# Modulation summed over whole rows of 2048 values, loaded two columns ahead, with its small sums once per block of 16

## The chip, the cores and the metric

The kernel runs on one core of one Trainium2 chip. The metric is the device time of one execution in microseconds. Engines are named as the profile names them: PE (TensorE, PEld is its weight load), DVE (VectorE), ACT (ScalarE), POOL (GpSimd) and SP (SyncE, which issues the loads).

## The reference

An encoder of two layers works on x of 256 tokens by 2048 features. Each layer is modulated by a vector c of 2048 values (adaLN):

```python
c_act = jax.nn.silu(c)
for l in range(DEPTH):
    mod = c_act @ ada_w[l] + ada_b[l]                     # 2048 -> 6 * 2048
    sh1, sc1, g1, sh2, sc2, g2 = jnp.split(mod, 6)
    h = rmsnorm(x, norm_mix_g[l]) * (1.0 + sc1) + sh1
    proj = h @ w_in[l] + b_in[l]
    y = concat(rglru(...), attention(...), hyena(...), mlstm(...))   # the mixer, four groups of 512 features
    x = x + g1 * (y @ w_out[l])
    h = rmsnorm(x, norm_ffn_g[l]) * (1.0 + sc2) + sh2
    x = x + g2 * swiglu(h, ffn_w1[l], ffn_w3[l], ffn_w2[l])
return rmsnorm(x, final_g)
```

All arrays are float32. The modulation alone reads 2 x 2048 x 12288 weights, 201 MB; the large products read the rest.

## The kernel before

The stream x lies in SBUF as 16 tiles of 128 features by 256 tokens. All large weights come from HBM in pieces of 128 x 1024 values (512 KB) through SP's queue into three `raw` buffers. Each piece is split exactly into two float32r parts: ACT makes `hi` (L335), DVE makes `lo` = raw - hi (L336), with three buffers of each. PE then runs 24 matmuls of 128 x 256 per piece: `hi` by `hi` of the activation (L372), `hi` by its `lo` (L373), and `lo` by its `hi` (L374). The result is collected in the banks `a`. DVE adds it to the stream, times a column of the modulation (`x`, L1097, two tiles per bank). ACT squares x (`sq`), PE sums the squares (`ss`, L475), and the root comes back spread over the partitions as `rb` (L482). The normed input `h` is made tile by tile: DVE multiplies x, a factor `g` and `rb` (L495), ACT adds the shift and rounds (L497), DVE makes the rest (L498).

The modulation has 192 columns: 2 layers, 6 parts (0 to 5 are sh1, sc1, g1, sh2, sc2, g2), 16 columns of 128 features each. A column is 128 dot products of 2048 values, one to a partition, of a block of `ada` weights with `cb`, which holds silu(c) on every partition. DVE does it with a multiplication that accumulates along the row (L423; the profile shows a `DVE_READ_ACCUMULATOR` behind each). Before, a column is done in two halves of 1024 values, each with a load of 512 KB of its own. A load and its sum stand together in the program:

```python
self.load(t, self.d["ada"][l, b, :, h * 1024:(h + 1) * 1024])
nc.vector.scalar_tensor_tensor(t, t, 1.0, self.cb[:, h * 1024:(h + 1) * 1024], ALU.mult, ALU.mult,
                               accum_out=self.acc[l][:, b, h:h + 1])
```

The halves go into two buffers `ada` of 4 KB a partition, and at the start of the program two of three go into spare tiles of another pool, `ad`. After the second half one small sum per column (L428) adds the halves and the bias; for parts 2 and 5 two small sums per 16 columns do (L432, L433). The norm's factor g = (1 + sc) * norm weight is one more small instruction per tile (L493).

The columns are strewn among the weights: after each piece `ada(rate)` is called, with the rates `RATES` in half columns a piece, for w_in, the first w1 and w3, the rest of the feed-forward part, and w_out. The first 32 columns (layer 0, parts 0 and 1) are needed at the start, where the spectra of the hyena filters are made. A call `modc` asks for a column and makes what is still missing.

A scheduler puts the instructions of each engine into order from a simulated timeline, and each engine then works in that order. `load` holds a load behind the weights that were asked for before it (`issue_after`).

Of the kernel before, what the change touches and what calls it, by code (L numbers as in the profile page):

```python
# [18 lines left out]
P = 128  # L19
DEPTH = 2  # L20
# [24 lines left out]
def _in_columns():  # L45
    """Source column of every column of the 42 plain blocks, in the kernel's order."""
# [22 lines left out]
def _out_rows():  # L69
    """Source row of w_out for every row of the mixed features, in the kernel's order c, d, a, b."""  # L70
    r = [1024 + np.arange(1024), np.arange(512)]
    for i in range(4):
        r += [512 + 64 * i + np.arange(64), 512 + 64 * (i + 4) + np.arange(64)]
    return np.concatenate(r)
# [5 lines left out]
# ---------------------------------------------------------------- constants of the shapes  # L80
def _constants():
# [36 lines left out]
    # behind the permutation of the rotation: rows 2 i and 2 i + 1 spread over the halves of tile i  # L118
# [38 lines left out]
# ---------------------------------------------------------------- layout of the inputs  # L157
# [67 lines left out]
# ---------------------------------------------------------------- the program  # L225
# pairs of column blocks that are worked on together while their input is still being made
IN_LEAD, OUT_LEAD, FFN_LEAD = 4, 5, 3
# half columns of the modulation per piece of weights, by layer: w_in, first w1 and w3, the rest of the FFN, w_out
# [3 lines left out]
class Lazy:  # L232
    """A list of n tiles, each made when it is first asked for, in their order."""
# [13 lines left out]
class Net:  # L247
    NRAW, NHL, NADA = 3, 3, 2
    # 2 KB tiles, by what they hold: a tag's tiles get their places in the order of the program
# [57 lines left out]
    def load(self, dst, src):  # L307
        """A load that does not run ahead of the weights that were asked for before it."""
# [47 lines left out]
    def product(self, banks, acts, m):  # L356
        """bank[:, b*T:(b+1)*T] = W[:, block b].T @ act, for m blocks of 128 columns in each bank.
        acts: per row tile, [hi | lo]. Several banks take turns chunk by chunk."""
# [18 lines left out]
    def products(self, n, lead, acts):  # L377
        """The banks of n pairs of column blocks in turn; the first `lead` of them are worked on together."""
# [8 lines left out]
    def split(self, dst, src):  # L387
        """dst (float32r) = [hi | lo] of src, exactly."""
        self.nc.scalar.activation(dst[:, :T], src, AF.Copy)  # L389
        self.nc.vector.tensor_tensor(dst[:, T:], src, dst[:, :T].bitcast(F32), ALU.subtract)  # L390

# [1 line left out]
    def ada_init(self, order):  # L393
# [11 lines left out]
        self.acc = [self.cp.tile([P, 96, 2], F32, name=f"acc{l}") for l in range(DEPTH)]  # L405
        self.ada_items = [(l, b, h) for l, b in order for h in range(2)]
        self.ada_at = 0
        self.ada_left = 0.0

    def ada(self, n, wide=False):  # L410
        """The next n half columns of the modulation; wide: with more of them under way."""
        nc = self.nc
        self.ada_left += n
        while self.ada_left >= 0.999 and self.ada_at < len(self.ada_items):
            self.ada_left -= 1
            l, b, h = self.ada_items[self.ada_at]
            self.ada_at += 1
            if wide and self.ada_at % 3:
                t = self.pair("ad")
            else:  # L420
                t = self.wp.tile([P, 1024], F32, tag="ada", name=self.nm("ada"), bufs=self.NADA)
            self.load(t, self.d["ada"][l, b, :, h * 1024:(h + 1) * 1024])
            nc.vector.scalar_tensor_tensor(t, t, 1.0, self.cb[:, h * 1024:(h + 1) * 1024], ALU.mult, ALU.mult,  # L423
                                           accum_out=self.acc[l][:, b, h:h + 1])
            if h == 0:
                continue
            if b // 16 not in (2, 5):
                nc.vector.scalar_tensor_tensor(self.mod[l][:, b:b + 1], self.acc[l][:, b, 0:1], self.acc[l][:, b, 1:2],  # L428
                                               self.pc(l, "ada_b", b), ALU.add, ALU.add)
            elif b % 16 == 15:  # L430
                m = self.mod[l][:, b - 15:b + 1]
                nc.vector.tensor_tensor(m, self.acc[l][:, b - 15:b + 1, 0], self.acc[l][:, b - 15:b + 1, 1], ALU.add)  # L432
                nc.vector.tensor_tensor(m, m, self.pc(l, "ada_b", b - 15, 16), ALU.add)  # L433

    def modc(self, l, j, k):
        """Column k of part j; parts 2 and 5 come as a whole."""
        b = j * 16 + k
        while self.ada_at <= self.ada_items.index((l, b | 15 if j in (2, 5) else b, 1)):
            self.ada(1, wide=l == 0 and j < 2)
        return self.mod[l][:, b:b + 1]  # L440

# [1 line left out]
    def rsqrt(self, v, n):  # L443
        """v ** -0.5 of a tiny tile: a start from ScalarE, one Newton step on it."""
# [743 lines left out]
```

## Time and profile before

| | us |
|---|---|
| time, median of 3 runs | 2658.27 |
| lowest and highest run | 2654.43, 2661.93 |
| span of the profiled execution (its own time, from the first to the last instruction) | 2648.9 |
| PE busy in it | 2523.5 |
| DVE busy | 1811.4 |
| ACT busy | 1158.7 |

The span leaves out what lies around the instructions, so the timed runs stand 5.5 to 13.0 us above it. A busy PE counts its matmuls at their own pace, with the granted clock in them; an engine that waits off PE's path costs nothing.

### The profile page before, as it was taken

The numbers are of one execution on the slowest core, as the hardware profiler recorded it, in microseconds if no ns is written. First come the engines' busy times: TensorE is split into PE (matmuls) and PEld (weight loads), VectorE is DVE, ScalarE is ACT, GpSimd is POOL, SyncE is SP. The second block draws the span as 40 slices with busy tenths as digits, with TensorE's granted clock in tenths as the row PEclk, the third lists the DMA queues.
The fourth block names the chain that finished last, engine by engine and source line by source line (L and its number), as shares of the span: only waits on it lengthen the run. The fifth ranks groups of instructions, "written<-read, shape, count | busy, mean of one in ns | idle before, by whom it ended". The sixth has DMA issues, their size and how long they took to land.

```text
span 2648.9 us, 47579 instructions
## 1 busy us (share of the span) xinstructions
PE 2523.5 (95%) x19410; PEld 2404.3 (91%) x19410; DVE 1811.4 (68%) x2778; ACT 1158.7 (44%) x1669; POOL 161.9 (6%) x142
## 2 busy tenths in 40 slices
PE   6889989798999999999998999999899999999998
PEld 3469989598999999999998898989899999999998
DVE  7888788778767666766677767777766454454445
ACT  4444455444443344334434445654444334433443
POOL 2101010021000000000020111002000000000001
PEclk9789999898999999999999999999999999999999
DMA  8787878467887778887776766658688656556654
GB/s 281 267 308 267 263 255 295 173 244 241 278 281 272 263 267 266 271 265 269 254 257 231 254 219 229 212 167 271 223 282 270 192 183 183 180 181 189 183 180 148
DMA packets 180752, 630.19 MB, mean 238 GB/s; under 512 B 20162, under 2 KB 20371, under 8 KB 180531
## 3 DMA queue, kind: packets, MB, share of 16 engines
q1 hardware_dynamic: 177076, 620.84, 70.5%
q10 hardware_dynamic: 3456, 6.29, 0.6%
q8 instruction: 152, 2.49, 0.4%
q14 instruction: 68, 0.56, 0.1%
HBM read 618.67 MB, written 8.39 MB: 237 GB/s over the span
## 4 chain that ended last, share of the span: by engine, by line
PE 58%; DMA 8%; DVE 5%; issue 4%; ACT 1%; SPq 0%; POOL 0%; DVEq 0%; POOLq 0%; ACTq 0%
PE a L374 19%; PE a L373 19%; PE a L372 19%; DMA ada<-in_ada 6%; DVE lo L336 2%; DMA raw<-in_w_in 1%; DMA raw<-in_w 1%; DVE ada L423 1%; ACT hi L335 0%; DMA raw<-in_w_out 0%; DVE x L1097 0%; DVE h L495 0%; DVE h L498 0%; SPq L324 0%; PE m L812 0%
## 5 line engine op out<-in xcount | busy, mean ns | idle before, releaser
L335 ACT ACTIVATE hi<-raw 128x1024 fp32r<-128x1024 f32 (+2 forms) x780 | 810.8, 1041 | 1181.4 <-PE a L373 698.5
L336 DVE TENSOR_TENSOR lo<-raw,hi 128x1024 fp32r<-128x1024 f32 (+2 forms) x780 | 948.1, 1218 | 425.1 <-ACT hi L335 419.9
L374 PE MATMUL a<-h,lo 128*128 128x256 f32 x4192 | 1204.2, 288 | 26.7 <-DVE lo L336 26.6
L372 PE MATMUL a<-h,hi 128*128 128x256 f32 x4192 | 1206.0, 288 | 10.2 <-ACT hi L335 5.5
L373 PE MATMUL a<-h,hi 128*128 128x256 f32 x4192 | 1206.3, 288 | 1.7 <-DVE h L498 1.7
L374 PEld LDWEIGHTS a<-h,lo 128*128 128x128 f32 x4192 | 815.1, 195 | 40.6 <-DVE lo L336 30.2
L372 PEld LDWEIGHTS a<-h,hi 128*128 128x128 f32 x4192 | 815.7, 195 | 28.5 <-ACT hi L335 8.9
L373 PEld LDWEIGHTS a<-h,hi 128*128 128x128 f32 x4192 | 815.5, 195 | 8.1 <-DVE h L498 2.8
L423 DVE SCALAR_TENSOR_TENSOR ada<-ada,cb 128x1024 f32<-128x1024 f32 x341 | 425.1, 1247 | 340.7 <-DMA ada<-in_ada 339.9
L374 PE MATMUL a<-g,lo 128*128 128x256 f32 x1408 | 399.7, 284 | 2.9 <-DVE lo L336 2.8
L373 PE MATMUL a<-g,hi 128*128 128x256 f32 x1408 | 399.2, 283 | 0.0
L372 PE MATMUL a<-g,hi 128*128 128x256 f32 x1408 | 399.1, 283 | 0.0
L374 PEld LDWEIGHTS a<-g,lo 128*128 128x128 f32 x1408 | 271.0, 193 | 4.0 <-DVE lo L336 4.0
L372 PEld LDWEIGHTS a<-g,hi 128*128 128x128 f32 x1408 | 271.1, 193 | 0.0
L373 PEld LDWEIGHTS a<-g,hi 128*128 128x128 f32 x1408 | 271.0, 192 | 0.0
L466 POOL TENSOR_TENSOR sq<-sq,sq 128x256 f32<-128x256 f32 x65 | 81.6, 1255 | 1694.4 <-issue 1399.7
L1097 DVE SCALAR_TENSOR_TENSOR x<-a,mod,x 128x256 f32<-128x256 f32 x128 | 55.8, 477 | 5.5 <-PE a L374 5.4
L423 DVE SCALAR_TENSOR_TENSOR ad<-ad,cb 128x1024 f32<-128x1024 f32 x43 | 54.5, 1274 | 0.1
L389 ACT ACTIVATE g<-s 128x256 fp32r<-128x256 f32 x88 | 35.9, 408 | 35.2 <-DVE s L1109 35.1
L497 ACT ACTIVATE h<-h,mod 128x256 fp32r<-128x256 f32 x64 | 29.4, 501 | 42.0 <-DVE h L495 28.5
L464 ACT ACTIVATE sq<-x 128x256 f32<-128x256 f32 x75 | 29.2, 413 | 24.5 <-DVE x L1097 24.3
L374 PE MATMUL a<-yc,lo 128*128 128x256 f32 x128 | 36.8, 288 | 1.0 <-DVE lo L336 1.0
(247 smaller groups left out, 2017.7 us busy)
## 6 DMA issues: line engine op xcount, KB each, us to landing
raw<-in_w SPq DMA_DIRECT2D x496, 512.0 KB, 4.6
ada<-in_ada SPq DMA_DIRECT2D x341, 512.0 KB, 5.7
raw<-in_w_in SPq DMA_DIRECT2D x168, 512.0 KB, 4.9
raw<-in_w_out SPq DMA_DIRECT2D x64, 512.0 KB, 5.7
ad<-in_ada SPq DMA_DIRECT2D x43, 512.0 KB, 6.3
raw<-in_w SPq DMA_DIRECT2D x32, 384.0 KB, 3.1
spectra<-sl ACTq DMA_DIRECT2D x24, 256.0 KB, 7.0
spec<-spectra SPq DMA_DIRECT2D x24, 256.0 KB, 6.7
```

Of the source, the lines that this page charges most:

```text
L335: self.nc.scalar.activation(hi[:, :n], t[:, :n], AF.Copy)
L336: self.nc.vector.tensor_tensor(lo[:, :n], t[:, :n], hi[:, :n].bitcast(F32), ALU.subtract)
L372: mm(o, hi[:, c], a[:, :T], start=first and b == 0, stop=False, skip_group_check=True)
L373: mm(o, hi[:, c], a[:, T:], start=False, stop=False, skip_group_check=True)
L374: mm(o, lo[:, c], a[:, :T], start=False, stop=last, skip_group_check=True)
L389: self.nc.scalar.activation(dst[:, :T], src, AF.Copy)
L423: nc.vector.scalar_tensor_tensor(t, t, 1.0, self.cb[:, h * 1024:(h + 1) * 1024], ALU.mult, ALU.mult, accum_out=self.acc[l][:, b, h:h + 1])
L464: nc.scalar.activation(t, self.x[k], AF.Square)
L466: nc.gpsimd.tensor_tensor(self.sq, self.sq, t, ALU.add)
L497: nc.scalar.activation(h[:, :T], t, AF.Identity, bias=sh)
L1097: self.nc.vector.scalar_tensor_tensor(self.x[k], ps[:, b * T:(b + 1) * T], g, self.x[k], ALU.mult, ALU.add)
```

## The change

A column is now one load of 1 MB (128 x 2048) and one sum over 2048 values. There are three buffers of 8 KB a partition, and the load of a column is asked for two columns ahead of its sum. The tiles `ad` and the argument `wide` are gone. Only layer 0's parts 0 and 1 keep one small instruction per column: for part 1 it makes the factor (`gain`) at once, for part 0 the shift. Everywhere else the bias is added once per 16 columns, and for the scale parts (1 and 4) a second instruction makes the 16 factors; L493 is gone. The order of the columns is now by whole parts, apart from layer 0's parts 1 and 0. `modc` waits for the whole block of 16 where it is made at once. The scratch size given to the compiler makes room in SBUF.

```diff
-    NRAW, NHL, NADA = 3, 3, 2
+    NRAW, NHL, NADA = 3, 3, 3
...
-        self.acc = [self.cp.tile([P, 96, 2], F32, name=f"acc{l}") for l in range(DEPTH)]
-        self.ada_items = [(l, b, h) for l, b in order for h in range(2)]
-        self.ada_at = 0
+        self.acc = [self.cp.tile([P, 96], F32, name=f"acc{l}") for l in range(DEPTH)]
+
+        self.gain = {(l, j): self.cp.tile([P, 16], F32, name=f"gain{l}{j}") for l in range(DEPTH) for j in (1, 4)}
+        self.bias1 = self.cp.tile([P, 16], F32, name="bias1")
+        nc.vector.tensor_scalar(self.bias1, self.pc(0, "ada_b", 16, 16), 1.0, None, ALU.add)
+        self.ada_items = order
+        self.ada_at = self.ada_got = 0
         self.ada_left = 0.0
-
-    def ada(self, n, wide=False):
-        """The next n half columns of the modulation; wide: with more of them under way."""
+        self.ada_tiles = {}
+
+    def ada(self, n):
+
         nc = self.nc
         self.ada_left += n
-        while self.ada_left >= 0.999 and self.ada_at < len(self.ada_items):
-            self.ada_left -= 1
-            l, b, h = self.ada_items[self.ada_at]
+        while self.ada_left >= 1.999 and self.ada_at < len(self.ada_items):
+            self.ada_left -= 2
+            while self.ada_got < min(len(self.ada_items), self.ada_at + self.NADA):
+                l, b = self.ada_items[self.ada_got]
+                t = self.wp.tile([P, D], F32, tag="ada", name=self.nm("ada"), bufs=self.NADA)
+                self.load(t, self.d["ada"][l, b])
+                self.ada_tiles[self.ada_got] = t
+                self.ada_got += 1
+            l, b = self.ada_items[self.ada_at]
+            t = self.ada_tiles.pop(self.ada_at)
             self.ada_at += 1
...
-            nc.vector.scalar_tensor_tensor(t, t, 1.0, self.cb[:, h * 1024:(h + 1) * 1024], ALU.mult, ALU.mult,
-                                           accum_out=self.acc[l][:, b, h:h + 1])
...
+            acc, mod = self.acc[l], self.mod[l]
+            nc.vector.scalar_tensor_tensor(t, t, 1.0, self.cb, ALU.mult, ALU.mult, accum_out=acc[:, b:b + 1])
+            j, k = b // 16, b % 16
+            if l == 0 and j < 2:
+                if j:
+                    nc.vector.scalar_tensor_tensor(self.gain[l, j][:, k:k + 1], acc[:, b:b + 1], self.bias1[:, k:k + 1],
+                                                   self.pc(l, "nmix", k), ALU.add, ALU.mult)
+                else:
+                    nc.vector.tensor_tensor(mod[:, b:b + 1], acc[:, b:b + 1], self.pc(l, "ada_b", b), ALU.add)
+            elif k == 15:
+                c = slice(j * 16, j * 16 + 16)
+                nc.vector.tensor_tensor(mod[:, c], acc[:, c], self.pc(l, "ada_b", j * 16, 16), ALU.add)
+                if j in (1, 4):
+                    nc.vector.scalar_tensor_tensor(self.gain[l, j], mod[:, c], 1.0, self.pc(l, "nmix" if j == 1 else "nffn", 0, 16),
+                                                   ALU.add, ALU.mult)
...
         b = j * 16 + k
-        while self.ada_at <= self.ada_items.index((l, b | 15 if j in (2, 5) else b, 1)):
-            self.ada(1, wide=l == 0 and j < 2)
-        return self.mod[l][:, b:b + 1]
...
+        while self.ada_at <= self.ada_items.index((l, b if l == 0 and j < 2 else b | 15)):
+            self.ada(2)
+        return self.gain[l, j][:, k:k + 1] if j in (1, 4) else self.mod[l][:, b:b + 1]
...
-                g = self.yp.tile([P, 1], F32, tag="g", name=self.nm("g"))
-                nc.vector.scalar_tensor_tensor(g, sc, 1.0, self.pc(l, gname, k), ALU.add, ALU.mult)
...
-        order = [(l, j * 16 + k) for l in range(DEPTH) for js in ((1, 0), (2,), (4, 3), (5,)) for k in range(16) for j in js]
+        order = [(0, j * 16 + k) for k in range(16) for j in (1, 0)]
+        order += [(l, j * 16 + k) for l in range(DEPTH) for j in ((1, 0) if l else ()) + (2, 4, 3, 5) for k in range(16)]
...
-    nc = bacc.Bacc("TRN2", target_bir_lowering=False, num_devices=1)
+    nc = bacc.Bacc("TRN2", target_bir_lowering=False, num_devices=1, dynamic_dma_scratch_size=1024)
```

The scheduler's order moves with it. On SP, in layer 0's mixer at the rate of one half column a piece, these loads stand in a row before:

```order
L313 DMA ada_1667<-in_ada 128x1024
L324 DMA raw_1670<-in_w_in 128x1024
L313 DMA ada_1700<-in_ada 128x1024
L324 DMA raw_1703<-in_w_in 128x1024
L313 DMA ada_1733<-in_ada 128x1024
L324 DMA raw_1736<-in_w_in 128x1024
```

and these in the changed kernel, at about the same place:

```order
L324 DMA raw_1549<-in_w_in 128x1024
L313 DMA ada_1579<-in_ada 128x2048
L324 DMA raw_1582<-in_w_in 128x1024
L324 DMA raw_1612<-in_w_in 128x1024
L313 DMA ada_1642<-in_ada 128x2048
L324 DMA raw_1648<-in_w_in 128x1024
```

The same bytes go in one load after every second piece. In layer 0's attention DVE makes the rotated `aq` in steps that alternate with PE (L758 and L762 to L767 before, L767 and L771 to L776 after). Before, DVE has there:

```order
L758 SCALAR_TENSOR_TENSOR aq_3998<-p_3710,par,m_4047 128x512
L423 SCALAR_TENSOR_TENSOR ada_5002,acc_151<-ada_5002,cb 128x1024
L428 SCALAR_TENSOR_TENSOR mod_149<-acc_151,par 128x1
L493 SCALAR_TENSOR_TENSOR g_6233<-mod_149,par 128x1
L762 TENSOR_TENSOR aa_4050<-m_4052,rope_3988 128x512
L423 SCALAR_TENSOR_TENSOR ada_5066,acc_151<-ada_5066,cb 128x1024
L767 TENSOR_TENSOR aq_3998<-aq_3998,aa_4050 128x512
L758 SCALAR_TENSOR_TENSOR aq_3999<-p_3710,par,m_4057 128x512
L762 TENSOR_TENSOR aa_4060<-m_4062,rope_3988 128x512
L767 TENSOR_TENSOR aq_3999<-aq_3999,aa_4060 128x512
```

and after, for the same steps:

```order
L767 SCALAR_TENSOR_TENSOR aq_3787<-p_3515,par,m_3836 128x512
L336 TENSOR_TENSOR lo_4664<-raw_4661,hi_4663 128x1024
L771 TENSOR_TENSOR aa_3839<-m_3841,rope_3777 128x512
L336 TENSOR_TENSOR lo_4697<-raw_4694,hi_4696 128x1024
L767 SCALAR_TENSOR_TENSOR aq_3788<-p_3515,par,m_3846 128x512
L431 SCALAR_TENSOR_TENSOR ada_4754,acc_151<-ada_4754,cb 128x2048
L776 TENSOR_TENSOR aq_3787<-aq_3787,aa_3839 128x512
L771 TENSOR_TENSOR aa_3849<-m_3851,rope_3777 128x512
L776 TENSOR_TENSOR aq_3788<-aq_3788,aa_3849 128x512
```

Two half sums stood between the steps, and one whole sum and two `lo` stand there now; on PE 65 weight matmuls stand between the first step of these (L755, now L764) and the scores (L783, now L792), where 18 stood. At the change from layer 0 to layer 1 DVE has before:

```order
L423 SCALAR_TENSOR_TENSOR ada_14885,acc_152<-ada_14885,cb 128x1024
L432 TENSOR_TENSOR mod_150<-acc_152 128x16
L336 TENSOR_TENSOR lo_14870<-raw_14867,hi_14869 128x1024
L433 TENSOR_TENSOR mod_150<-mod_150,par 128x16
L1097 SCALAR_TENSOR_TENSOR x<-a_14773,mod_149,x 128x256 x2
L336 TENSOR_TENSOR lo_14945<-raw_14942,hi_14944 128x1024
L423 SCALAR_TENSOR_TENSOR ada_15002,acc_152<-ada_15002,cb 128x1024
L478 TENSOR_SCALAR v_14903<-ss_14896 128x2
```

and after:

```order
L431 SCALAR_TENSOR_TENSOR ada_14219,acc_152<-ada_14219,cb 128x2048
L336 TENSOR_TENSOR lo_14234<-raw_14231,hi_14233 128x1024
L336 TENSOR_TENSOR lo_14264<-raw_14261,hi_14263 128x512
L336 TENSOR_TENSOR lo_14294<-raw_14291,hi_14293 128x1024
L336 TENSOR_TENSOR lo_14324<-raw_14321,hi_14323 128x1024
L1106 SCALAR_TENSOR_TENSOR x<-a_14230,mod_149,x 128x256 x2
L431 SCALAR_TENSOR_TENSOR ada_14339,acc_152<-ada_14339,cb 128x2048
L489 TENSOR_SCALAR v_14356<-ss_14349 128x2
```

The sum ahead of the layer's last stream update (L1097, now L1106) moved up by four `lo`; between it and the norm's `v` a `lo` and a half sum became one whole sum. At the end of layer 0's w_out a whole sum and two `lo` stand ahead of the last `x`, at the end of layer 1's a whole sum alone.

## Rows read from the trace of the kernel before

**Rows 1.** Page: busy time of each engine; the chain that ended last, by line.

```profile
PE 2523.5 (95%) x19410; PEld 2404.3 (91%) x19410; DVE 1811.4 (68%) x2778; ACT 1158.7 (44%) x1669; POOL 161.9 (6%) x142
...
PE a L374 19%; PE a L373 19%; PE a L372 19%; DMA ada<-in_ada 6%; DVE lo L336 2%; DMA raw<-in_w_in 1%; DMA raw<-in_w 1%; DVE ada L423 1%; ACT hi L335 0%; DMA raw<-in_w_out 0%; DVE x L1097 0%; DVE h L495 0%; DVE h L498 0%; SPq L324 0%; PE m L812 0%
```

**Rows 2.** Groups on ACT and DVE: xcount, busy us, mean ns, idle before.

```profile
L335 ACT ACTIVATE hi<-raw 128x1024 fp32r<-128x1024 f32 (+2 forms) x780 | 810.8, 1041 | 1181.4 <-PE a L373 698.5
L336 DVE TENSOR_TENSOR lo<-raw,hi 128x1024 fp32r<-128x1024 f32 (+2 forms) x780 | 948.1, 1218 | 425.1 <-ACT hi L335 419.9
...
L423 DVE SCALAR_TENSOR_TENSOR ada<-ada,cb 128x1024 f32<-128x1024 f32 x341 | 425.1, 1247 | 340.7 <-DMA ada<-in_ada 339.9
...
L428 DVE SCALAR_TENSOR_TENSOR mod<-acc,par 128x1 f32<-128x1 f32 x128 | 32.2, 252 | 1.4
L423 DVE DVE_READ_ACCUMULATOR ada<-ada,cb 128x1 f32 x341 | 27.8, 81 | 0.0
...
L493 DVE SCALAR_TENSOR_TENSOR g<-mod,par 128x1 f32<-128x1 f32 x64 | 11.1, 178 | 0.3
```

**Rows 3.** Stretches: PE, PEld, DVE, ACT, POOL busy; clock, DMA share, GB/s.

```profile
0.00:195.00 195.00, 157.82 (x552) 94.17 (x553) 161.27 (x329) 83.05 (x160) 31.87 (x30) 0.89 0.82 284
195.00:484.00 289.00, 271.50 (x2018) 259.30 (x2017) 236.81 (x411) 146.44 (x242) 23.05 (x25) 0.97 0.80 272
484.00:534.00 50.00, 36.37 (x170) 22.68 (x169) 31.62 (x77) 18.93 (x50) 4.11 (x3) 0.76 0.33 115
...
595.00:637.00 42.00, 32.48 (x238) 30.81 (x237) 33.41 (x59) 15.44 (x22) 7.01 (x5) 0.88 0.81 274
637.00:1400.00 763.00, 759.42 (x6294) 758.20 (x6293) 528.66 (x720) 315.17 (x382) 18.38 (x13) 1.00 0.79 265
1400.00:1420.00 20.00, 12.24 (x76) 11.38 (x75) 14.78 (x35) 6.70 (x12) 0.70 (x1) 0.74 0.61 206
```

**Rows 4.** Waits of PE, then ACT, 637 to 1400: total, times, longest.

```profile
PE a L374 <- DVE lo L336: 3.5, 5, 1.9
...
ACT hi L335 <- DMA raw<-in_w: 176.6, 92, 4.2
```

**Rows 5.** Timeline of DVE at the start: start us, us, instruction.

```profile
28.49 1.21 DVE L423 SCALAR_TENSOR_TENSOR ada<-ada,cb 128x1024 f32<-128x1024 f32 x1
...
29.64 0.21 DVE L428 SCALAR_TENSOR_TENSOR mod<-acc,par 128x1 f32<-128x1 f32 x1
29.77 0.14 DVE L478 TENSOR_SCALAR v<-ss 128x2 f32<-128x2 f32 x1
```

**Rows 6.** Timeline at the layer change: DVE, then PE.

```profile
1405.33 1.23 DVE L423 SCALAR_TENSOR_TENSOR ada<-ada,cb 128x1024 f32<-128x1024 f32 x1 [2.70 <-DMA ada<-in_ada]
...
1407.93 0.87 DVE L1097 SCALAR_TENSOR_TENSOR x<-a,mod,x 128x256 f32<-128x256 f32 x2
...
1403.56 0.28 PE L374 MATMUL a<-g,lo 128*128 128x256 f32 x1
1403.68 0.50 PE L475 MATMUL ss<-misc,sq 128*128 128x1 f32 x4
1408.98 1.87 PE L475 MATMUL ss<-misc,sq 128*128 128x1 f32 x8 [4.79 <-ACT sq L464]
```

**Rows 7.** Timeline in layer 0's attention: DVE, then PE.

```profile
498.91 1.21 DVE L423 SCALAR_TENSOR_TENSOR ada<-ada,cb 128x1024 f32<-128x1024 f32 x1
...
503.25 1.22 DVE L423 SCALAR_TENSOR_TENSOR ada<-ada,cb 128x1024 f32<-128x1024 f32 x1 [1.41 <-DMA ada<-in_ada]
...
499.04 2.07 PE L760 MATMUL m<-aq,perm 128*128 128x512 f32 x2 [2.74 <-DVE aq L758]
```

**Rows 8.** Waits of PE in the whole kernel: total, times, longest.

```profile
PE a L374 <- DVE lo L336: 31.8, 23, 7.7
PE ss L475 <- ACT sq L464: 12.6, 4, 4.8
```

**Rows 9.** L423 alone by stretches: DVE busy us (instructions).

```profile
637.00:1400.00 763.00, 156.76 (x251) 1.00 0.79 265
```

More of the change, by code (lines that the diff above doesn't have):

```diff
@@ L408, in ada_init @@
+        nc.vector.tensor_scalar(self.bias1, self.pc(0, "ada_b", 16, 16), 1.0, None, ALU.add)
+        self.ada_items = order
+        self.ada_at = self.ada_got = 0
         self.ada_left = 0.0
-    def ada(self, n, wide=False):
+        self.ada_tiles = {}
+    def ada(self, n):
         nc = self.nc
         self.ada_left += n
-        while self.ada_left >= 0.999 and self.ada_at < len(self.ada_items):
-            self.ada_left -= 1
-            l, b, h = self.ada_items[self.ada_at]
-            self.ada_at += 1
[L418 to L422, printed above, removed]
-            nc.vector.scalar_tensor_tensor(t, t, 1.0, self.cb[:, h * 1024:(h + 1) * 1024], ALU.mult, ALU.mult,
-                                           accum_out=self.acc[l][:, b, h:h + 1])
[L425 to L433, printed above, removed]
@@ L483, in rstd, with norm @@
         return pb[:, :T]
-    def norm(self, l, gname, jsh, jsc):
+    def norm(self, l, jsh, jsc):
         nc = self.nc
@@ L489, in make @@
         def make(k):
-            sc, sh = self.modc(l, jsc, k), self.modc(l, jsh, k)
+            g, sh = self.modc(l, jsc, k), self.modc(l, jsh, k)
             with self.tc.high_priority(offset=50):
-                g = self.yp.tile([P, 1], F32, tag="g", name=self.nm("g"))
-                nc.vector.scalar_tensor_tensor(g, sc, 1.0, self.pc(l, gname, k), ALU.add, ALU.mult)
                 t = self.tmp("h")
@@ L569, in early @@
     def early(self, n):
-        self.ada(min(n, 64 - self.ada_at), wide=True)
-        k = min(self.ada_at // 4, KT)
+        self.ada(min(n, 64 - 2 * self.ada_at))
+        k = min(self.ada_at // 2, KT)
         if k:
@@ L1153, in run @@
         self.weights(self.weight_items())
-        self.ada(4, wide=True)
-        self.h0 = h = self.norm(0, "nmix", 0, 1)
+        self.ada(4)
+        self.h0 = h = self.norm(0, 0, 1)
         self.early(4)
@@ L1161, in run @@
         for l in range(DEPTH):
-            h = h or self.norm(l, "nmix", 0, 1)
+            h = h or self.norm(l, 0, 1)
             self.rate = RATES[l][0] if l else 0
@@ L1166, in run @@
             self.add_to_stream(l, y, 2, True, OUT_LEAD)
-            h = self.norm(l, "nffn", 3, 4)
+            h = self.norm(l, 3, 4)
             self.ffn(l, h)
```

## The prediction

> **What bounds the kernel now.** I read the page first: busy times and the chain that ended last; then the stretches by stage; then TensorE's waits; then the timeline at the places where TensorE stands. TensorE (PE) is busy for 2523.5 of 2648.9 us, and the three kinds of weight matmuls make up 57% of the chain [rows 1]. But the same chain gives 6% to transfers of modulation rows, `ada<-in_ada`, and in the groups the sums of L423 wait 339.9 us for them [rows 1, 2]. The reader has to hold these two against each other: VectorE (DVE) waiting is a loss only where PE then stands.
>
> The stretches decide that [rows 3]. In the feed-forward part of layer 0 (637 to 1400 us) PE is busy for 759.42 of 763 us at full clock. There the sums wait for their rows too, yet PE's waits for `lo` come to 3.5 us [rows 4]. Nothing in that stretch can be won back by quicker sums, and by the span it is 29% of the time. PE stands elsewhere: 195 − 157.82 = 37 us at the start, 17.5 in layer 0's mixer, 13.6 in the attention stretch (484 to 534), 9.5 and 7.8 around the ends of layer 0's w_out and w2 [rows 3], and the rest in the same places of layer 1. In all 2648.9 − 2523.5 = 125 us; that is the whole field. I go through these places.
>
> **What a sum costs.** One half row takes DVE 1247 ns on average with an accumulator read of 81 ns behind it [rows 2], but the work is pipelined: in a run of sums one starts 1.15 us after the other (28.49, and the next instruction at 29.64) [rows 5]. 1024 values at the rate of a large instruction and a fixed part make up that 1.15. For the fixed part I take the accumulator read, 0.08 us, so a row of 2048 costs 2 × 1.15 − 0.08 = 2.22 us. Bounds: nothing saved (2.30), and the whole pace of an instruction on a single value, L428's 0.13 (29.64 to 29.77), which can hold little but the fixed part. The saving per row is thus 0.08 us (0 to 0.13), over 192 rows 15 us of DVE (0 to 25), nearly all of it under PE.
>
> The Trainium skill, "VectorE: DVE Perf Modes", section on the errata, says that operations on SBUF pay a fixed latency per instruction, so that one large tile pays it once, and gives (N+151)/0.96 ns for an fp32 tensor operation: 1224 ns for 1024 values, which agrees with the 1.21 us of the row [rows 5], and 2291 ns for 2048. By those durations a row would save 157 ns, twice my figure; the row of successive sums shows that part of a duration overlaps the next instruction, so I stay with the pace.
>
> **The small instructions.** L428 (128 of them, 252 ns each) and L493 (64, 178 ns) [rows 2] cost 0.13 us of pace for the one [rows 5], half its duration, and by the same half 0.09 for the other. For layer 0's parts 0 and 1 one small instruction per column stays (L435 or L438), so 32 of the L428 stay in another form; the other 96, the 64 L493 and the four L432/L433 pairs shrink to one or two per block of 16. That is 96 × 0.13 + 64 × 0.09 = 18 us of DVE, again mostly under PE.
>
> **The terms.**
> *Start (0 to 195 us).* DVE is busy 161 of 195 us and PE follows the spectra and the first norm [rows 3]. 32 columns are summed here. Saved on DVE: 32 × 0.08 = 2.6 us and 16 × 0.09 = 1.4 us of L493. Since DVE is the busiest engine here, I count all of it: **−4 us** (0, if other waits take it up, to −6 with 0.13 a row).
> *Attention of layer 0.* PE waits 2.74 us for `aq` at 499.04; on DVE two sums stand between the steps of `aq`, at 498.91 and, after 1.41 us of waiting for its row, at 503.25 [rows 7]. That chain goes DVE, PE, DVE, so each sum counts: 1.41 wait + 2 × 1.15 + L428 and L493, 0.2. After, by the order, one sum of 2.2 us still stands between these steps, with rows that were asked for two columns ahead, and it stands before a step whose input is there; 47 more weight matmuls (65 for 18) stand between the steps on PE, 5.6 us of work. I take **−4 us** (+1, if the longer sum falls on the chain, to −10, if the matmuls fill most of the 13.6 us).
> *Ends of w_out and w2.* At the layer change PE's last weight matmul and four `ss` products end at 1404.2, and the next `ss` starts at 1408.98, after 4.79 us. The stream update `x` could have started at about 1404.2 but stood on DVE behind a sum that waited 2.70 us for its row (to 1405.33), a `lo` and two small sums until 1407.93 [rows 6]. After, the sum is several rows ahead of `x`, with its row loaded early. From `x` to `ss` is 1408.98 − 1407.93 = 1.05 us, so a wait of some 1.25 us must stay. PE waits so 4 times, 12.6 us [rows 8]; what can go is 12.6 − 4 × 1.25 = 7.6 us. At the end of layer 0's w_out, by the order, a 2.2 us sum and two `lo` stand close ahead of `x`, so I take **−6 us** (0 to −7.6).
> *Mixers.* PE's waits for `lo` come to 31.8 us in the whole kernel, 23 of them [rows 8]; these `lo` wait on DVE for their turn or for `hi`. Shorter waits of sums ahead of `lo` may help, a sum of 2.2 us ahead of a late `lo` may hurt by 2.22 − 1.15 = 1.1 us each time, over 23 such waits at most 25 us. I take **−1 us** (−6 to +8).
> *Loads.* 192 issues go from SP. A row now takes twice the transfer in one piece ahead of the weights behind it. Weights are late already at times: ScalarE waits 176.6 us for `raw` in the feed-forward part of layer 0, up to 4.2 us, and PE hardly notices [rows 4]. A half row of 512 KB at the 265 GB/s of that stretch [rows 3] is 2.0 us, so a weight may come up to 2.0 us later than now every second time; the hi and lo buffers hold two pieces ahead, worth 2 × 24 × 0.12 (759.42 us for 6294 matmuls) = 5.8 us of PE, less 1.04 + 1.22 for making `hi` and `lo` [rows 2], 3.5 us. I take **+1 us** (0 to +25).
> *Scratch size and `bias1`:* one small instruction, nothing.
>
> Sum: −4 − 4 − 6 − 1 + 1 = −14 us on the execution profiled, 2648.9 to 2634.9. The median of the three runs, 2658.27, is 9.4 us above that span, and I carry this over: **2644.3 us**, 0.5% faster.
>
> **The rivals.**
> *A. No change.* Within 0.3%, 8 us, about what a measurement of this kernel can tell from no change. The sums wait under PE's work, as in the feed-forward part, and the ends of the products move little, since one long sum stands before `x` in place of two short ones. For it: PE's share of 95% [rows 1]. Against: the 4.79 us at the layer change plainly ends on a late row [rows 6]. It gives 2 us at the start and 1 at the other places: 2655 us.
> *B. Large gain.* If transfers of 1 MB with 8 KB in a row keep the queues better filled, the stages that transfers hold (start at 284 GB/s, mixer of layer 0 at 272, engines 0.8 busy [rows 3]) get shorter; PE idle there is 37 + 17.5 us, and a third of it with my sum gives 2658.3 − 14 − 18 = 2626 us. Against: PE's waits in these stages go mostly to `lo` and to small chains, not to transfers. The Trainium skill, "DMA: Bandwidth & Descriptors", rules for kernel authors, asks for 1 MiB or more per DMA; no row here shows a transfer of that size, and by its rule this rival would win.
> *C. Slower.* The 1 MB rows ahead of the weights, in the feed-forward part of layer 0. Some 63 rows are loaded there (251 instructions of L423 stand in that stretch, two for a half row [rows 9]). The longest ScalarE wait, 4.2, with 2.0 on top is 6.2 us against my 3.5 to 5.8 us of cover, so PE could stand after each late one. At 0.6 us a row the price is 38 us, and 2644.3 + 38 = 2682 us; it decides from about 0.35 us a row (22 us, the 14 of gain and the 8 that can be told). Against: the mean traffic there is the same, the engines are 0.79 busy [rows 3], and loads are asked for earlier.
>
> **How the numbers follow.** My forecast 0.52, A 0.25, B 0.08, C 0.15. The likeliest gives 2644.3. Mixers at their bad end (+9 against my −1), attention at its own (+5) and loads at a third of theirs (+8) give 2666 as the upper end; A lies inside, most of C is left out. Downwards all terms at their good ends (−6 − 10 − 7.6 − 6 = −30 us) give 2628, and B's middle lies at 2626, so the low end is 2622. About 2 in 10 stay outside. Faster by over 0.3%: the forecast less its weak end, 0.47, and B, 0.08: 0.55. Within 0.3%: A and 0.05 of the forecast, less 0.03 that ends slower: 0.27. Slower: 0.18.
>
> **What would show it.** Sums of about 2.29 us, 2.2 us apart at the start; DVE's wait for `ada` far below 339.9 us with the feed-forward stretches as long as before; the first `ss` after each w_out and w2 after less than 2 us; the two sums gone from the chain of `aq`. I am wrong if PE waits for `lo` or `hi` in the feed-forward part of layer 0 by more than some 10 us, or if the norms at the ends start no earlier.

## The result and the profile after

The changed kernel takes 2696.9 us (median of 4 runs, 2696.7 to 2698.6), beside 2660.1 us for the kernel before in the same runs: 1.015 times as long, with a 95% interval of 1.0136 to 1.0164. The prediction was 2644.3, with a range of 2622 to 2666. It is slower, by more than the prediction's rival C gave (2682), and in the stage that this rival named, but, as the runs below show, not by the mechanism that it gave. A run that stands far above the others of its kernel (there is one, 5019.3 us with two loads) is left out of the times and ratios below.

The page of the changed kernel (busy times, then groups as in [rows 2], then DMA issues with KB and median us to landing):

```profile
PE 2536.7 (94%) x19410; PEld 2411.9 (89%) x19410; DVE 1765.8 (66%) x2240; ACT 1159.9 (43%) x1669; POOL 169.9 (6%) x142
...
L336 DVE TENSOR_TENSOR lo<-raw,hi 128x1024 fp32r<-128x1024 f32 (+2 forms) x780 | 946.8, 1223 | 611.4 <-ACT hi L335 599.2
...
L431 DVE SCALAR_TENSOR_TENSOR ada<-ada,cb 128x2048 f32<-128x2048 f32 x192 | 442.8, 2307 | 223.6 <-DMA ada<-in_ada 220.1
...
raw<-in_w SPq DMA_DIRECT2D x496, 512.0 KB, 4.5
ada<-in_ada SPq DMA_DIRECT2D x192, 1024.0 KB, 7.4
```

DVE's busy time fell by 46 us and its waits for modulation rows from 339.9 [rows 2] to 220.1 us, as the prediction wanted. By those two lines alone the change looks like a success. The stretches (columns as in [rows 3], cut at the same places of the program) say where the time went:

```profile
0.00:198.00 198.00, 156.22 (x511) 90.08 (x512) 153.49 (x248) 79.51 (x152) 37.96 (x30) 0.89 0.78 280
486.00:536.00 50.00, 40.24 (x209) 26.82 (x208) 30.98 (x65) 21.20 (x53) 4.07 (x3) 0.80 0.30 108
626.00:1449.00 823.00, 782.18 (x6340) 773.63 (x6340) 517.97 (x566) 319.12 (x389) 19.43 (x13) 0.98 0.71 249
1449.00:1469.00 20.00, 13.84 (x96) 13.00 (x96) 18.59 (x36) 10.02 (x19) 1.61 (x1) 0.83 0.42 138
```

The feed-forward part of layer 0, from the first weight matmul on `h` to the end of the last on `g`, took 1403.84 − 632.98 = 770.9 us before and takes 1449.06 − 625.91 = 823.2 now. That is 52 us in a stage where PE had stood for 4 us, as the same stretch of the kernel before shows:

```profile
633.00:1404.00 771.00, 766.87 (x6340) 765.36 (x6340) 535.12 (x736) 318.27 (x388) 18.38 (x13) 0.99 0.78 264
```

PE stands there for 823 − 782 = 41 us now, 37 us more, and the same 6340 matmuls keep it busy for 782.18 − 766.87 = 15 us longer. Part of the 15 us is the granted clock, 0.98 for 0.99. Behind the first microseconds of the stage it falls to 0.50 (1.2 GHz) six times, for 3.4 us each, during or up to 2 us after a wait of PE of 1.3 to 2.6 us, though not with every such wait; before, it did so once. One such stretch of the changed kernel, 1 us after PE had waited 2.29 us for a `lo`:

```profile
1245.60:1248.80 3.20, 3.20 (x17) 3.20 (x16) 1.50 (x2) 0.14 (x1) 0.00 (x0) 0.50 0.71 214
```

The stage begins 7 us earlier than before, so what lies ahead of it gained a little.

What PE waits for there (waits of PE, then of DVE, then of ACT, 626 to 1449 us, as in [rows 4]):

```profile
PE a L374 <- DVE lo L336: 35.4, 30, 2.6
...
DVE ada L431 <- DMA ada<-in_ada: 130.5, 50, 5.1
...
ACT hi L335 <- DMA raw<-in_w: 342.1, 161, 4.3
```

PE's waits for `lo` went from 3.5 [rows 4] to 35.4 us. Two readings offer themselves. ACT's waits for weights (`raw`) doubled from 176.6 [rows 4], as if the long rows held the weights up on the queue. Or DVE's waits for a row, which are 2.6 us long on average and up to 5.1, hold up the `lo` behind them. One of PE's waits, in the timeline of DVE, then ACT, SP's issues and PE:

```profile
1198.59 2.29 DVE L431 SCALAR_TENSOR_TENSOR ada<-ada,cb 128x2048 f32<-128x2048 f32 x1 [4.04 <-DMA ada<-in_ada]
1200.81 0.08 DVE L431 DVE_READ_ACCUMULATOR ada<-ada,cb 128x1 f32 x1
1200.81 1.22 DVE L336 TENSOR_TENSOR lo<-raw,hi 128x1024 fp32r<-128x1024 f32 x1
...
1194.19 1.06 ACT L335 ACTIVATE hi<-raw 128x1024 fp32r<-128x1024 f32 x1 [0.90 <-DMA raw<-in_w]
...
1199.78 1.06 ACT L335 ACTIVATE hi<-raw 128x1024 fp32r<-128x1024 f32 x1 [4.26 <-DMA raw<-in_w]
...
1189.49 0.43 SPq L313 DMA_DIRECT2D ada<-in_ada  x1
1190.51 13.34 SPq L324 DMA_DIRECT2D raw<-in_w  x4
...
1202.08 0.39 PE L374 MATMUL a<-h,lo 128*128 128x256 f32 x1 [2.30 <-DVE lo L336]
```

Read it from the `hi` at 1194.19. It is made by 1195.25, and its `lo` could follow. But the next instruction on DVE is a sum whose row was asked for at 1189.49 and lands at 1198.59. DVE stands for 4.04 us, sums for 2.2, and starts the `lo` at 1200.81, 5.6 us after its `hi` was made. PE has run out of work at 1199.78 and stands for 2.30 us, until the `lo` is there. In the same time SP's four `raw` issues take 13.34 us, since a `raw` buffer comes free only when a `lo` has read it: so the weights of the following pieces are late too, and ACT waits 4.26 us for one. Of the 30 waits of PE for `lo` in the stage 29 look like this: followed back on DVE without a gap, the `lo` leads to a sum that waited for its row. The late weights may be a consequence then.

### The profile page after: what moved, and what is told of

The parts are those of the page before. It is cut to its first block, busy times and chain, and to the rows that moved or that the text cites. A ratio compares the mean times of both kernels' runs of the same rounds, so it can differ in the third digit from the quotient of the medians.

```text
span 2695.1 us, 46749 instructions
## 1 busy us (share of the span) xinstructions
PE 2536.7 (94%) x19410; PEld 2411.9 (89%) x19410; DVE 1765.8 (66%) x2240; ACT 1159.9 (43%) x1669; POOL 169.9 (6%) x142
## 5 line engine op out<-in xcount | busy, mean ns | idle before, releaser
L374 PE MATMUL a<-h,lo 128*128 128x256 f32 x4192 | 1210.5, 290 | 53.7 <-DVE lo L336 53.2
L431 DVE SCALAR_TENSOR_TENSOR ada<-ada,cb 128x2048 f32<-128x2048 f32 x192 | 442.8, 2307 | 223.6 <-DMA ada<-in_ada 220.1
L1106 DVE SCALAR_TENSOR_TENSOR x<-a,mod,x 128x256 f32<-128x256 f32 x128 | 55.9, 479 | 6.1 <-PE a L374 6.1
L1118 DVE TENSOR_TENSOR s<-s,a 128x256 f32<-128x256 f32 x88 | 36.6, 415 | 0.9 <-ACT s L1117 0.9
L1067 ACT ACTIVATE p<-a,par 128x256 f32<-128x256 f32 x76 | 31.6, 467 | 12.5 <-PE a L374 12.4
```

The lines of the kernel that those rows point to most:

```text
L374: mm(o, lo[:, c], a[:, :T], start=False, stop=last, skip_group_check=True)
L431: nc.vector.scalar_tensor_tensor(t, t, 1.0, self.cb, ALU.mult, ALU.mult, accum_out=acc[:, b:b + 1])
L1067: nc.scalar.activation(o[:, c], ps[:, c], func, bias=self.pc(l, "b_in", k))
L1106: self.nc.vector.scalar_tensor_tensor(self.x[k], ps[:, b * T:(b + 1) * T], g, self.x[k], ALU.mult, ALU.add)
L1118: nc.vector.tensor_tensor(s, s, ps[:, T:], ALU.mult)
```

## The experiments

Theory 1: a `lo` stands in DVE's order behind a sum whose row has not landed, and wait and sum together exceed the cover (the 3.5 us of PE's work that the prediction's term *Loads* worked out for the `hi` and `lo` made ahead). Theory 2: whole rows on SP's queue make the weights late. Theory 3: the 2.29 us of a whole sum in front of a `lo` do it. All ratios are to the kernel before in the same runs, with their 95% intervals; "the stage" is the feed-forward part of layer 0, measured as above (770.9 us before, 823.2 after).

**Sums held.** In DVE's order (rows word for word, without their numbers) the changed kernel has

```
L336 TENSOR_TENSOR lo_7453<-raw_7450,hi_7452 128x1024
L1118 TENSOR_TENSOR s_7443<-s_7443,a_7319 128x256
L431 SCALAR_TENSOR_TENSOR ada_7480,acc_151<-ada_7480,cb 128x2048
```

while SP has

```
L324 DMA raw_7450<-in_w 128x1024
L313 DMA ada_7480<-in_ada 128x2048
L324 DMA raw_7483<-in_w 128x1024
```

The sum stands behind the `lo` of the very piece that was asked for just ahead of its row. Two columns of look-ahead in the program have become none in the order. It is so throughout: counted in the orders of SP and DVE in the trace, 62 of the stage's 63 sums stand here or one `lo` earlier, on average 7.7 us behind the issue of their row. The kernel before puts 120 of its 126 half sums in the same places, 6.1 us behind. The edit ties each sum behind the newest `lo`:

```diff
+            self.last_lo = self.nc.vector.tensor_tensor(lo[:, :n], t[:, :n], hi[:, :n].bitcast(F32), ALU.subtract).ins
...
+            with (self.tc.issue_after(self.last_lo) if self.last_lo is not None else ExitStack()):
+                nc.vector.scalar_tensor_tensor(t, t, 1.0, self.cb, ALU.mult, ALU.mult, accum_out=acc[:, b:b + 1])
```

> The changed kernel, but each sum is held on DVE behind the newest lo that the program has asked for at that point, so that its row was asked for 2 to 8 pieces of weights earlier (in the changed kernel it stands 1 to 4 pieces ahead of the weights that were asked for before its row). Theory 1, a lo stands on DVE behind a sum whose row has not landed: DVE's waits for rows in the feed-forward part of layer 0 fall from 129 us to under 15, PE's waits for lo there from 34.6 to under 6, and the time falls by 40 to 55 us, to 2642 to 2657. Theory 2, whole rows on SP's queue make the weights late: the loads have the same size and rate, so ACT's waits for raw stay over 300 us, PE goes on waiting, and the time stays over 2685.

Measured: 2636.2 us, 0.992 (0.990 to 0.994), 6 us below the range of theory 1. The stage takes 764.0 us, and its sums now stand 5 to 9 `lo` behind the piece asked for ahead of their row, on average 31 us after it was asked for. Its waits from 629 to 1393 us, the largest in total of PE and of DVE, and ACT's for weights:

```profile
PE a L372 <- ACT h L508: 1.2, 1, 1.2
...
DVE lo L336 <- ACT hi L335: 241.2, 188, 3.2
...
ACT hi L335 <- DMA raw<-in_w: 102.8, 46, 4.0
```

No wait of PE for `lo` is left, nor one of DVE for a row. With the same 1 MB loads in the same queue ACT's waits for weights fell from 342.1 to 102.8 us. Theory 2 falls: the late weights were the consequence. Theory 3 falls too, as these sums are as long as in the changed kernel and PE does not wait behind them. The prediction's range, 2622 to 2666, holds the time of this kernel.

**Two loads.**

```diff
-                self.load(t, self.d["ada"][l, b])
+                for h in range(2):
+                    self.load(t[:, h * 1024:(h + 1) * 1024], self.d["ada"][l, b, :, h * 1024:(h + 1) * 1024])
```

> The changed kernel with each row fetched by two loads of 512 KB, one behind the other, and one sum over the whole row. Theory 1: the sum stands at the same place and needs both halves, so nothing changes by more than 10 us: 2687 to 2707. Theory 2 in the form that transfers of 8 KB in a partition are what slows the queue: back to 2655 to 2670.

Measured: 2727.6 us, 1.027 (1.024 to 1.029), above the range of either theory; the stage takes 843.7 us. The size of one transfer is not what slowed the kernel. Two issues in place of one make it worse: DVE's waits for rows in the stage are 149.9 us in 56 times.

**Half sums.** One load of a whole row, two sums of 1024 values, each with an accumulator of its own.

```diff
+            for h, a in enumerate((acc, self.acc2[l])):
+                u = t[:, h * 1024:(h + 1) * 1024]
+                nc.vector.scalar_tensor_tensor(u, u, 1.0, self.cb[:, h * 1024:(h + 1) * 1024], ALU.mult, ALU.mult, accum_out=a[:, b:b + 1])
```

> The changed kernel with whole rows loaded, but each summed in two halves of 1024 values (and one more small addition per column in layer 0's parts 0 and 1, per 16 columns elsewhere). Theory 1: both halves wait for the same load, the wait is what counts: 2690 to 2705. Theory 3, the 2.29 us of a whole sum in front of a lo is the cause: a lo can go between the halves, and the time falls to 2660 to 2680.

Measured: 2687.8 us, 1.011 (1.009 to 1.014), just under the range of theory 1. The stage is hardly better, 816.4 us. That says little about theory 3, since DVE's order left the halves together: behind a row that it waited for, 1.9 half sums follow on average before the next `lo`. But the start is better: the last of layer 0's first sixteen `h` is done at 188.5 us here, at 198.2 in the changed kernel and at 186.7 before. There the length of a sum does cost some 10 us.

**Half rows in pairs.** As the half sums, and each half in a buffer and a load of its own (six buffers of 4 KB); both halves of a column are still asked for and summed together.

```diff
-                t = self.wp.tile([P, D], F32, tag="ada", name=self.nm("ada"), bufs=self.NADA)
-                self.load(t, self.d["ada"][l, b])
+                t = []
+                for h in range(2):
+                    u = self.wp.tile([P, 1024], F32, tag="ada", name=self.nm("ada"), bufs=2 * self.NADA)
+                    self.load(u, self.d["ada"][l, b, :, h * 1024:(h + 1) * 1024])
+                    t.append(u)
```

> The changed kernel with half rows again: loads of 512 KB into six buffers of 4 KB, sums of 1024 values, still asked for two columns ahead in the program, the small sums and factors still once per block. Theory 1: the scheduler still puts each sum right behind its load, but a half row lands sooner (5.5 us for 7.4), so DVE waits less: the feed-forward part costs 0 to 15 us more than in the kernel before, the gains at the ends of the products stay, 2645 to 2665. Theory 2: the same or slightly better, 2645 to 2660. If the batching of the small sums or the order of the columns were the cause, it would stay over 2685.

Measured: 2705.7 us, 1.019 (1.015 to 1.022): a miss of 40 us, for both theories, and a time at which the expectation would blame the batching or the order of the columns; two runs below settle that. The stage takes 811.8 us although rows and sums are as short as before. What was left over were the batching, the order of the columns, the asking ahead and the pairs.

**Half rows in pairs, held.** The same with the hold.

```diff
+                with (self.tc.issue_after(self.last_lo) if self.last_lo is not None else ExitStack()):
+                    nc.vector.scalar_tensor_tensor(u, u, 1.0, self.cb[:, h * 1024:(h + 1) * 1024], ALU.mult, ALU.mult, accum_out=a[:, b:b + 1])
```

> Half rows in six buffers, asked for two columns ahead, and each half sum held on DVE behind the newest lo. Theory 1, the place of the sum in DVE's order is what counts and not the size of a row: as the changed kernel with held sums, 2636 within 6 us. If whole rows are worth something of their own (fewer fixed parts, fuller transfers): 2645 or more.

Measured: 2621.0 us, 0.986 (0.985 to 0.988); the stage takes 768.7 us. Below the expected range, and 15 us below the held whole rows: a size of its own does count, against whole rows.

**Sums of 8 values.** The changed kernel, each sum over the first 8 of its 2048 values; the rest of the sums is left out.

```diff
-            nc.vector.scalar_tensor_tensor(t, t, 1.0, self.cb, ALU.mult, ALU.mult, accum_out=acc[:, b:b + 1])
+            nc.vector.scalar_tensor_tensor(t[:, :8], t[:, :8], 1.0, self.cb[:, :8], ALU.mult, ALU.mult, accum_out=acc[:, b:b + 1])
```

> The changed kernel in which a sum reads only 8 of its row's 2048 values (the rest of each sum is left out); loads and waits stay. Theory 1 with the wait alone as price: a lo still stands behind a late row, DVE's waits for rows stay at 100 us or more in the feed-forward part of layer 0, and the time falls only by what DVE's work is worth, to 2675 to 2690. Theory 1 with wait and sum together against the 3.5 us of cover: without the 2.2 us most waits stay under the cover, PE's waits for lo there fall from 34.6 to under 10, and the time is 2640 to 2660.

Measured: 2571.3 us, 0.968 (0.965 to 0.970); the stage takes 765.7 us. Waits in it, of PE, then DVE (572 to 1338 us):

```profile
PE a L374 <- DVE lo L336: 1.6, 2, 1.0
...
DVE ada L431 <- DMA ada<-in_ada: 164.5, 60, 4.8
```

DVE waits for rows longer than in the changed kernel (164.5 for 130.5 us), and PE does not notice. So the wait alone is not the price either; wait and sum together are. That the total came 69 us below the low end of the expectation shows a second thing: outside of the stage DVE's sums are on PE's path. The start ends at 170.5 us for 198.2, and the stage begins at 572.2 for 625.9.

**Halves one at a time, not ahead** (two buffers, as before, with the changed kernel's order of columns and small sums). Beside halves as in the pairs above:

```diff
-        while self.ada_left >= 1.999 and self.ada_at < len(self.ada_items):
-            self.ada_left -= 2
-            while self.ada_got < min(len(self.ada_items), self.ada_at + self.NADA):
+        while self.ada_left >= 0.999 and self.ada_at < 2 * len(self.ada_items):
+            self.ada_left -= 1
+            while self.ada_got < min(2 * len(self.ada_items), self.ada_at + 1):
```

> The kernel before in loads and sums (half rows, one at a time in two buffers, asked for where they are summed), with the changed kernel's order of columns, its small sums and factors once per block. Theory 1: the transfers are spread as before, so no new waits; some DVE work saved: 2650 to 2662. If batching or the order of the columns costs time: 2675 or more.

Measured: 2709.1 us, 1.020 (1.018 to 1.023), a miss, but a plain one: the start ends at 243.6 us, most likely since the kernel before had spare tiles `ad` there and this one only two buffers. From there on it goes as the kernel before: the stage takes 770.1 us for 770.9. Batching and the order of the columns cost the stage nothing.

**Halves one at a time, ahead** (six buffers; the edit is shown against the run above).

```diff
-            while self.ada_got < min(2 * len(self.ada_items), self.ada_at + 1):
+            while self.ada_got < min(2 * len(self.ada_items), self.ada_at + 6):
```

> As the run with halves one at a time, but asked for five halves ahead into six buffers, still one at a time. It differs from the half rows in pairs (2706 us) only in that the two halves of a column are no longer asked for and summed together. If the burst of 1 MB per column is the cause: 2645 to 2665. If asking ahead itself is the cause (loads taken up earlier by the scheduler, sums right behind them): 2690 or more.

Measured: 2645.8 us, 0.997 (0.995 to 0.999); the stage takes 774.1 us. Waits there, of PE, then DVE (628 to 1402 us):

```profile
PE a L374 <- DVE lo L336: 7.7, 8, 2.3
...
DVE ada L433 <- DMA ada<-in_ada: 165.7, 108, 4.2
```

This settles the half rows in pairs: it is the pair. The reader can now put the stops side by side. A stop is the mean wait for a row and the sums that follow on it without a `lo` between, from the stage's waits of each kernel:

| kernel | waits for rows in the stage | mean stop, us | PE's waits for `lo`, us |
|---|---|---|---|
| before | 154.9 in 108 | 1.4 + 1.15 = 2.6 | 3.5 |
| halves one at a time, ahead | 165.7 in 108 | 1.5 + 1.15 = 2.7 | 7.7 |
| sums of 8 values | 164.5 in 60 | 2.7 + 0.1 = 2.8 | 1.6 |
| half rows in pairs | 138.6 in 73 | 2.2 + 2.1 = 4.3 | 33.1 |
| after | 130.5 in 50 | 2.6 + 2.2 = 4.8 | 35.4 |
| half sums | 122.7 in 48 | 2.6 + 2.2 = 4.8 | 31.0 |
| two loads | 149.9 in 56 | 2.7 + 2.2 = 4.9 | 53.2 |

The lines of the table that stand nowhere else (before, two loads, half sums, half rows in pairs; DVE, then PE):

```profile
DVE ada L423 <- DMA ada<-in_ada: 154.9, 108, 4.0
...
DVE ada L432 <- DMA ada<-in_ada: 149.9, 56, 5.2
PE a L374 <- DVE lo L336: 53.2, 41, 2.5
...
DVE ada L434 <- DMA ada<-in_ada: 122.7, 48, 5.3
PE a L374 <- DVE lo L336: 31.0, 26, 3.3
...
DVE ada L437 <- DMA ada<-in_ada: 138.6, 73, 4.4
PE a L374 <- DVE lo L336: 33.1, 35, 3.2
```

In the pairs some columns wait twice, and a stop holds 1.8 half sums on average. The total that DVE waits says nothing. The length of one stop against the prediction's cover of 3.5 us parts the seven kernels into those where PE waits for under 8 us and those where it waits for over 30; within the second group it does not put them in order.

**Four held kernels.** The hold is the same `issue_after` at each sum. Whole rows with half sums, held:

> Whole rows loaded in one transfer of 1 MB, each summed in two halves, the sums held behind the newest lo. It stands between the held whole sums (0.992 of before) and the held half rows (0.986). If the length of a sum on DVE makes their difference (at the start and in the mixers an urgent small instruction waits behind 2.2 us in place of 1.15): 0.984 to 0.989. If the size of the transfer makes it: 0.990 to 0.994.

Measured: 2617.2 us, 0.985 (0.982 to 0.988), as the held half rows. So it is the length of a sum, not of a transfer, that sets the held whole sums 15 to 19 us behind: their start ends at 199.9 us, this one's at 185.8. Halves one at a time, ahead, held:

> Half rows asked for one at a time, five halves ahead, the sums held. Without the hold, asking for the halves of a column together cost the feed-forward part of layer 0 some 35 us against asking one at a time. Theory 1: once no sum stands ahead of its row, this no longer matters: 0.984 to 0.989 of before, as the held half rows in pairs. If bursts cost something in themselves: below 0.982.

Measured: 2610.0 us, 0.982 (0.979 to 0.984); the stage takes 764.2 us. It is the fastest version that makes the whole sums, 87 us below the changed kernel. Its ratio lies below the range of theory 1, just inside the other reading, and its interval lies just below that of the pairs (0.985 to 0.988), whose stage takes 4.5 us more. So asking in pairs may still cost some us where no sum stands ahead of its row; 11 us by the medians, and not settled by these runs. The held half rows with small sums per column and factors per tile:

```diff
+                nc.vector.scalar_tensor_tensor(mod[:, b:b + 1], acc[:, b:b + 1], self.acc2[l][:, b:b + 1],
+                                               self.pc(l, "ada_b", b), ALU.add, ALU.add)
...
+                nc.vector.scalar_tensor_tensor(g, sc, 1.0, self.pc(l, "nffn" if jsc == 4 else "nmix", k), ALU.add, ALU.mult)
```

> The held half rows (0.986 of before) with the small sums per column and the norm's factors per tile again, as in the kernel before. The batching saves some 18 us of DVE's time by the prediction's working, mostly under PE: if that is worth nothing on PE's path, 0.985 to 0.989; if DVE's time counts at the start and in the mixers as it did when the sums were cut to 8 values (they gave back half of DVE's saving), 0.989 to 0.993.

Measured: 2629.9 us, 0.989 (0.986 to 0.992). By the medians the batching is worth 9 us, but the intervals overlap; inconclusive. The kernel before, only held:

```diff
+            with (self.tc.issue_after(self.last_lo) if self.last_lo is not None else ExitStack()):
+                nc.vector.scalar_tensor_tensor(t, t, 1.0, self.cb[:, h * 1024:(h + 1) * 1024], ALU.mult, ALU.mult,
+                                               accum_out=self.acc[l][:, b, h:h + 1])
```

> The kernel before with nothing changed but that each half sum is held behind the newest lo; loads are still asked for where they are summed, so a row is asked for just behind the weights of that lo. Theory 1: a hold without asking ahead leaves little time for the row, DVE's waits for rows fall by about half (from 340 us) and PE gains little: 0.990 to 1.000 of before. If the hold alone is the gain: 0.988 or less.

Measured: 2620.3 us, 0.986 (0.982 to 0.989). That misses what was worked out from theory 1 and agrees with the other reading: the hold alone is the gain. It gives as much as the held versions of the change do (0.982 to 0.992). The half sums now stand one `lo` later than before, right behind that of the piece asked for ahead of their row, and DVE's waits for rows fall from 339.9 [rows 2] not by half but to this, in the waits of DVE in the whole kernel:

```profile
DVE ada L425 <- DMA ada<-in_ada: 31.4, 36, 2.5
```

A row need not be asked for earlier if its sum is put a piece later.

## Why the prediction was wrong

*The sum.* Right. 2.22 us for a row of 2048 was the working; three in a row at the start begin 2.21 to 2.22 us apart (timeline of DVE):

```profile
23.39 2.29 DVE L431 SCALAR_TENSOR_TENSOR ada<-ada,cb 128x2048 f32<-128x2048 f32 x1 [1.49 <-ACT cb L403]
...
25.61 2.28 DVE L431 SCALAR_TENSOR_TENSOR ada<-ada,cb 128x2048 f32<-128x2048 f32 x1
...
27.82 2.28 DVE L431 SCALAR_TENSOR_TENSOR ada<-ada,cb 128x2048 f32<-128x2048 f32 x1
```

With [rows 5] that is 0.08 us saved per row. The Trainium skill's formula ("VectorE: DVE Perf Modes", errata) gave the duration well, 2291 for 2307 ns, but by it and the durations a row would save 157 ns, twice what the pace shows.

*Start, −4 us.* Wrong in sign: +11.5 us (198.2 for 186.7). DVE's work shrank as worked out, but with half sums on the same loads the start ends at 188.5, so a sum of 2.2 us in one piece costs about 10 us there. That short urgent work waits behind it is my explanation; which instruction it is was not separated. By 626 us it is won back: the feed-forward part begins 7 us earlier than before.

*Attention, −4 us.* Right in direction: PE's waits for `aq` fell from 7.2 to 3.5 us in the whole kernel, and the attention stretch has PE busy for 40.2 of 50 us for 36.4 [rows 3]. By the count of PE's weight matmuls it was more: from number 2000, ahead of the attention, to number 2300, behind it, PE took 84.2 us before and takes 75.1 now.

*Ends of w_out and w2, −6 us.* Right: PE's waits for `ss` (whole kernel, as in [rows 8]) came to

```profile
PE ss L486 <- ACT sq L475: 7.9, 4, 2.7
```

so 4.7 us of the 12.6 went, and the three gaps between the last weight matmul before a norm and the first after it shrank from 9.4, 10.1 and 8.8 to 8.7, 7.5 and 7.0 us, 5.1 in all.

*Loads, +1 us (0 to +25).* This is the step that failed, and with it the sentence that the sums have "rows that were asked for two columns ahead". The stage cost +52 us. The step priced whole rows as late weights, for which the cover sufficed. What the runs showed in its place is a stop of DVE, wait and whole sum together 4.8 us, ahead of a `lo` that was due, against the 3.5 us of cover that the same step had worked out, and that the seven kernels bear out (by them it lies between 2.8 and 4.3). The prediction's own sign of being wrong, more than some 10 us of PE's waits there, came out at 35.4. The term *Mixers* came near the cause with "a sum of 2.2 us ahead of a late `lo`", but counted 1.1 us of sum and no wait for the row; for the rest of the kernel it was about right, as outside of the stage PE's waits for `lo` went from 31.8 − 3.5 = 28.3 to 60.1 − 35.4 = 24.7 us:

```profile
PE a L374 <- DVE lo L336: 60.1, 48, 4.5
```

The order lists of the changed kernel, read for where a sum stands against its own load, show the missing look-ahead; I had read there only how sums and `x` stand to each other.

*Rival C* named the stage and, at 0.6 us a row, 38 us; with 63 rows it was 52/63 = 0.8. Its mechanism, weights behind 1 MB rows, is refuted by the held sums. *Rival B* found nothing for it: with the sums held and equally long, loads of 1 MB and of 512 KB give 0.985 and 0.986, and the start, which this rival named, ends at 185.8 us with either. The rule of 1 MiB or more per DMA for most bandwidth (the Trainium skill, "DMA: Bandwidth & Descriptors", rules for kernel authors) brought nothing here.

*The carry-over of 9.4 us* from span to median was mostly the spread of the runs: the changed kernel's profiled run took 2696.9 us for a span of 2695.1, 1.8 above it, and a run of the kernel before, beside the held sums, 2652.7 for 2650.9.

## What to carry to other kernels

On an engine that works in order, ask of each instruction that waits for a transfer where it stands against its own load and what stands behind it; a look-ahead in the program is worth nothing if the order puts the consumer right behind the load. Weigh one stop (wait and work together) against the cover of the engine behind, not the sum of all waits: the kernel with fewer stops and less waiting in all was slower. Before making transfers larger, try to put the consumer later; here that took a few lines, and gave 1.4% by itself.

## What was not expected

- DVE at 68% busy was on the path all the same outside of the feed-forward parts: without the work of the sums (179 of 2307 ns each) the time fell to 0.968 of before; layer 0's feed-forward part began 54 us earlier than in the changed kernel (572.2 for 625.9), and took no longer than before.
- The next instruction on DVE started 1.148 us after a sum of 1024 values (mean, before) and 2.215 us after one of 2048, so the part that does not grow with the length was 2 × 1.148 − 2.215 = 0.08 us, though a sum itself shows 1.21 or 2.29 us.
- A row of 1 MB landed in 7.4 us (median), one of 512 KB in 5.7 before: a row twice as long came 1.7 us later, and that with the longer sum was enough to pass the cover.
